# Four raw-weight buffers in place of two, in a one-core decoder trunk

## The chip, the core and the metric

The kernel runs on one core of a Trainium2 chip. The core has a matrix engine (TensorE, PE in the profile), a vector engine (VectorE, DVE), a scalar engine (ScalarE, ACT), a general engine (GpSimd, POOL) and a queue engine (SyncE, SP) that here only issues DMA transfers. Each runs its own list of instructions in order and waits on semaphores for the others. Sixteen DMA engines carry data between memory (HBM) and the on-chip buffer (SBUF, 128 partitions). Matrix products end in PSUM banks.

The metric is the device time of one execution in microseconds. Before the change the median of three runs is 2399.63 us (2398.58 to 2399.67).

## The reference

The input is one sequence of 512 vectors of 1024 float32 numbers, and a memory of 256 such vectors. Two layers follow each other. Each is: half a SwiGLU feed-forward step (FFN), a mixing step, half an FFN.

```python
def _swiglu(t, w_gate, w_up, w_down):
    return (jax.nn.silu(t @ w_gate) * (t @ w_up)) @ w_down
...
    for l in range(DEPTH):
        f = _swiglu(_rmsnorm(h, ffn1_pre_g[l]), ffn1_w_gate[l], ffn1_w_up[l], ffn1_w_down[l])
        h = h + 0.5 * _rmsnorm(f, ffn1_post_g[l])

        u = _rmsnorm(h, mix_pre_g[l])
        proj = u @ w_in[l]
...
        merged = (g_sb * (_merge_heads(o_sb) @ w_br_sb[l])
                  + g_fx * (_merge_heads(o_fx) @ w_br_fox[l])
                  + g_mem * (_merge_heads(o_mem) @ w_br_mem[l]))
        h = h + _rmsnorm(merged @ w_out[l], mix_post_g[l])

        f = _swiglu(_rmsnorm(h, ffn2_pre_g[l]), ffn2_w_gate[l], ffn2_w_up[l], ffn2_w_down[l])
        h = h + 0.5 * _rmsnorm(f, ffn2_post_g[l])
```

The FFN is 2816 wide (22 tiles of 128). The mixing step has eight heads of stick-breaking attention, eight of forgetting attention (a softmax with a decay) and four of attention to the memory, each gated by a sigmoid of a projection. All weights are float32 and are used once, so every weight comes from HBM in the course of the execution.

## The kernel before

**The arithmetic.** A float32 operand is split into a high part, rounded to the matrix engine's format, and the low part that remains. ScalarE makes the high part (line 188: `wh_...`, or 191 with a scale), VectorE subtracts it from the operand for the low part (line 189: `wl_...`, or 192). A product is then three matmuls of 128x128 by 128x512: high by high (line 214), low by high (215), high by low (216), added in PSUM. Activations are split in the same way.

**Units of weights.** Weights come in units of 512 KB: a `Unit` holds four row tiles by 256 columns, a `BlockUnit` two row tiles by 512 columns. `fetch` takes a tile with the tag "raw" and issues its DMA on SyncE's queue (line 262, and 313 for blocks); `load` makes the two halves and thereby frees the raw tile. A unit feeds 12 matmuls. The halves have four buffers each ("wh", "wl").

**Two by two blocks in seven products.** Most of the FFN's matrices are multiplied as two by two blocks by a scheme with seven block products in place of eight. Its operands are sums of blocks. Those of the weights are made on VectorE from a raw block and *kept* blocks (tiles kt for gate and up, bt for down), which are fetched on the same queue without the raw limit: product 2 subtracts a raw block from kept block 0 (line 337), product 3 takes the difference of the kept blocks (340), product 5 subtracts a raw block (345), product 6 as well (349); products 0 and 1 split a raw block as it is, and product 4 a kept block. In names, `wl_tc1_8_2_2` is the low part for FFN c1, group 8, product 2, second unit. The four FFNs are a0, c0, a1, c1 (layer 0 before and after mixing, layer 1 likewise), so the profile, which leaves numbers out, has ta, da, ga and tc, dc, gc.

**Stages of an FFN.** First two feature tiles, whose weights have buffers of their own, are multiplied plainly; then plain gate products of tiles 18 and 19 and the sums of the activations; then four groups of gate and up, of seven products each (the first in the order 0 to 6, the others 0, 2, 3, 4, 5, 1, 6), then two down products of seven each, with plain gate and up units of tiles 18 to 21 (named g..18, u..18, g..20, u..20) between, then the rest of down. In the first FFN the first group is followed by the statistics of the memory's norm (`mem_stats`, lines 1076 to 1084: squares and roots on ScalarE, which load activation tables). Between the FFNs the mixing stage multiplies plain units (w_in, gates wg and wb, w_out as wo, memory projections mk and mv) and runs the attention heads, whose exponentials and sums lie on ScalarE and VectorE.

**What sets the order.** A `Queue` holds jobs in program order. When a job starts, its units and those of the next jobs (up to four units ahead) are loaded. After each load, `fetch_ahead` goes through the jobs that follow and fetches raw units until as many are under way as the table `BUFS` has raw buffers (line 438); then it stops, and kept blocks of later units wait with it. So the count of raw buffers is used twice: in the tile pool, where a new raw tile waits for the tile that had its place, and here.

The lists that the engines run are not in the order of the program text: the build that allocates the tiles also places each engine's instructions by its own model of when each is ready. Only what `keep_in_program_order` or `in_order` (line 166) ties together keeps its order. On SyncE, each transfer that waits holds all that stand behind it.

**The scratch of dynamic transfers.** A part of SBUF is set aside for transfers that GpSimd issues. Its size is an argument of the program's constructor, left at its default here. The kernel has three such transfers, of small vectors, near the start: `bfor` (line 161) and two for `vecs` (lines 123 and 124), used in products at 62 us.

Of the kernel before, what the change touches and what calls it, by code (L numbers as in the profile page):

```python
# [22 lines left out]
def kernel(  # L23
# [38 lines left out]
    nc = tc.nc  # L62
# [37 lines left out]
    def tmp(name):  # L100
        return sb.tile([P, S], F32, tag="f32t", bufs=5, name=name)

    BUFS = {"u": 2, "v": 6, "q": 2, "k": 2, "o": 8, "tri": 2, "raw": 2, "rs": 1, "cs": 1, "wh": 4, "wl": 4, "f": 4}

    def stile(shape, tag, name, dt=F32R):
        return sb.tile(shape, dt, tag=tag, bufs=BUFS[tag], name=name)

# [264 lines left out]
    class Queue:  # L372
# [60 lines left out]
        def fetch_ahead(self):  # L433

            for units, _, _ in self.jobs[self.at:]:
                for un in units:
                    if un.waits():
                        if un.ring() and self.fetched == BUFS["raw"]:
                            return
# [1327 lines left out]
```

## Time and profile before

| | before |
|---|---|
| median of 3 runs | 2399.63 us |
| profiled execution, its own time | 2399.02 us |
| its span in the profile | 2397.3 us |
| TensorE busy | 2369.5 us, 99% |
| VectorE busy | 1870.9 us, 78% |
| ScalarE busy | 1399.4 us, 58% |
| GpSimd busy | 73.9 us, 3% |
| moved by DMA | 349.73 MB, 146 GB/s in the mean |
| share of the 16 DMA engines taken by SyncE's queue | 45.6% |
| granted TensorE clock | 0.999 |

The span runs from the first instruction to the last; the execution's own time has 1.7 us more, which lie outside it. The rows of a timeline have the start in us from the span's start, the duration in us, the engine, the line, the operation, output and inputs, and in brackets how long the engine had been idle before, and for what it waited. The rows of the waits have the engine, what waited, what ended the wait, and then the total in us, the number of times and the longest. "SPq" is SyncE's DMA queue.

### The profile page before, as it was taken

To read this page: it belongs to the slowest core of one execution; us is meant where nothing else is said; L and a number is where in the kernel's file an instruction comes from. 1 tells how busy PE (TensorE), PEld (TensorE's weight loads), DVE (VectorE), ACT (ScalarE), POOL (GpSimd) and SP (SyncE) were. 2 spreads that over 40 slices of the span, in tenths; PEclk is the share of its full clock that TensorE was granted. 3 is DMA by queue.
4 is the path that set the end of the run, shared out by engine and by line. 5 is a ranking of instruction groups with operands and counts; after the bars stand their busy time and mean duration, and the time that the engine had idled before them with its cause. 6 is when DMAs were issued, how large, how long until landed. Compare 5 with 4: busy or idle time off the path is not lost.

```text
span 2397.3 us, 31090 instructions
## 1 busy us (share of the span) xinstructions
PE 2369.5 (99%) x11688; PEld 1996.4 (83%) x11688; DVE 1870.9 (78%) x2532; ACT 1399.4 (58%) x2291; POOL 73.9 (3%) x130
## 2 busy tenths in 40 slices
PE   9999999999999999999999999999999999999998
PEld 8788788888888897888888887888888888888887
DVE  7778977678776687789787789776777766877895
ACT  5656555577665455565655565656675655555654
POOL 1000000001010000000000000000001100000000
PEclk9999999999999999999999999999999999999999
DMA  5464475222223445554645545642232244446454
GB/s 181 154 218 160 151 253 158 70 77 75 79 71 115 143 139 182 183 183 157 220 147 165 186 158 196 219 129 80 63 89 80 71 134 147 159 150 202 158 168 166
DMA packets 232603, 349.73 MB, mean 146 GB/s; under 512 B 10730, under 2 KB 117506, under 8 KB 231940
## 3 DMA queue, kind: packets, MB, share of 16 engines
q1 hardware_dynamic: 232352, 347.71, 45.6%
q8 instruction: 92, 1.51, 0.3%
q14 instruction: 59, 0.48, 0.1%
q0 software_dynamic: 96, 0.03, 0.0%
q10 hardware_dynamic: 4, 0.00, 0.0%
HBM read 333.02 MB, written 14.68 MB: 145 GB/s over the span
## 4 chain that ended last, share of the span: by engine, by line
PE 80%; DVE 8%; DMA 6%; ACT 3%; issue 2%; SPq 0%; DVEq 0%; ACTq 0%
PE pg L214 3%; PE pg L216 3%; PE pg L215 3%; PE ptc L215 3%; PE ptc L214 3%; PE ptc L216 3%; PE pta L214 3%; PE pta L215 3%; PE pta L216 3%; PE pdc L216 2%; PE pdc L215 2%; PE pdc L214 2%; PE pb L214 2%; PE pb L215 2%; PE pb L216 2%
## 5 line engine op out<-in xcount | busy, mean ns | idle before, releaser
L214 PE MATMUL pg<-us_a,wh_wg 128*128 128x512 f32 x384 | 151.0, 393 | 0.0
L216 PE MATMUL pg<-us_a,wl_wg 128*128 128x512 f32 x384 | 149.7, 390 | 0.0
L215 PE MATMUL pg<-us_a,wh_wg 128*128 128x512 f32 x384 | 149.6, 390 | 0.0
L188 ACT CAST wh_tc<-ktc 128x1024 fp32r<-128x1024 f32 x80 | 83.4, 1052 | 98.6 <-DVE ktc L349 34.1
L188 ACT CAST wh_ta<-kta 128x1024 fp32r<-128x1024 f32 x80 | 83.4, 1053 | 96.9 <-DVE kta L337 31.7
L189 DVE TENSOR_TENSOR wl_ta<-kta,wh_ta 128x1024 fp32r<-128x1024 f32 x80 | 97.1, 1222 | 29.8 <-ACT wh_ta L188 29.0
L189 DVE TENSOR_TENSOR wl_tc<-ktc,wh_tc 128x1024 fp32r<-128x1024 f32 x80 | 97.1, 1222 | 29.2 <-ACT wh_tc L188 28.4
L214 PE MATMUL pta<-wh_ta,aga 128*128 128x512 f32 x256 | 101.1, 397 | 4.5 <-ACT wh_ta L188 2.3
L214 PE MATMUL ptc<-wh_tc,agc 128*128 128x512 f32 x256 | 100.1, 393 | 3.1 <-ACT wh_tc L188 3.1
L215 PE MATMUL ptc<-wl_tc,agc 128*128 128x512 f32 x256 | 100.0, 391 | 1.5 <-DVE wl_tc L189 1.5
L215 PE MATMUL pta<-wl_ta,aga 128*128 128x512 f32 x256 | 100.2, 391 | 1.0 <-DVE wl_ta L189 1.0
L216 PE MATMUL pta<-wh_ta,aga 128*128 128x512 f32 x256 | 99.8, 391 | 0.0
L216 PE MATMUL ptc<-wh_tc,agc 128*128 128x512 f32 x256 | 99.4, 389 | 0.0
L215 PE MATMUL pda<-wl_da,aha 128*128 128x512 f32 x224 | 87.6, 391 | 0.8 <-DVE wl_da L189 0.8
L215 PE MATMUL pdc<-wl_dc,ahc 128*128 128x512 f32 x224 | 87.3, 390 | 0.5 <-DVE wl_dc L189 0.5
L214 PE MATMUL pda<-wh_da,aha 128*128 128x512 f32 x224 | 87.7, 391 | 0.1
L214 PE MATMUL pdc<-wh_dc,ahc 128*128 128x512 f32 x224 | 87.4, 390 | 0.0
L216 PE MATMUL pda<-wh_da,ala 128*128 128x512 f32 x224 | 86.9, 389 | 0.0
L216 PE MATMUL pdc<-wh_dc,alc 128*128 128x512 f32 x224 | 86.9, 389 | 0.0
L216 PEld LDWEIGHTS pg<-us_a,wl_wg 128*128 128x128 f32 x384 | 72.1, 188 | 15.3
L215 PEld LDWEIGHTS pg<-us_a,wh_wg 128*128 128x128 f32 x384 | 72.2, 188 | 14.1
L214 PEld LDWEIGHTS pg<-us_a,wh_wg 128*128 128x128 f32 x384 | 72.1, 188 | 14.1
(543 smaller groups left out, 7513.2 us busy)
## 6 DMA issues: line engine op xcount, KB each, us to landing
raw_ta<-in_ffn_w_gate_dram SPq DMA_DIRECT2D x64, 512.0 KB, 3.8
raw_tc<-in_ffn_w_gate_dram SPq DMA_DIRECT2D x64, 512.0 KB, 3.8
raw_da<-in_ffn_w_down_dram SPq DMA_DIRECT2D x58, 512.0 KB, 4.0
raw_dc<-in_ffn_w_down_dram SPq DMA_DIRECT2D x58, 512.0 KB, 3.5
raw_wg<-in_w_gate_dram SPq DMA_DIRECT2D x48, 512.0 KB, 3.6
kta<-in_ffn_w_up_dram SPq DMA_DIRECT2D x32, 512.0 KB, 5.4
ktc<-in_ffn_w_up_dram SPq DMA_DIRECT2D x32, 512.0 KB, 5.7
raw_wo<-in_w_out_dram SPq DMA_DIRECT2D x24, 512.0 KB, 3.4
```

What stands on the lines that cost most here:

```text
L188: both = [nc.scalar.copy(h_ap, src)]
L189: make = lambda: nc.vector.tensor_tensor(l_ap, src, h_ap.bitcast(F32), ALU.subtract)
L214: nc.tensor.matmul(pt, lh, rh, start=start, stop=False, skip_group_check=free)
L215: nc.tensor.matmul(pt, lh, rl, start=False, stop=False, skip_group_check=free)
L216: nc.tensor.matmul(pt, ll, rh, start=False, stop=stop, skip_group_check=free)
```

## The change

The raw tag has four buffers in place of two, so the pool holds four raw tiles of 4 KB per partition, and the limit on fetches under way (line 438) is four as well. The 8 KB per partition that this takes come from the scratch of dynamic transfers, which has 2 KB left. Nothing else in the text of the kernel differs; the order in which the build places the instructions of each engine is made anew.

```diff
-    BUFS = {"u": 2, "v": 6, "q": 2, "k": 2, "o": 8, "tri": 2, "raw": 2, "rs": 1, "cs": 1, "wh": 4, "wl": 4, "f": 4}
+    BUFS = {"u": 2, "v": 6, "q": 2, "k": 2, "o": 8, "tri": 2, "raw": 4, "rs": 1, "cs": 1, "wh": 4, "wl": 4, "f": 4}
...
-    nc = _bacc.Bacc("TRN2", target_bir_lowering=False, num_devices=1)
+    nc = _bacc.Bacc("TRN2", target_bir_lowering=False, num_devices=1, dynamic_dma_scratch_size=2048)
```

## The prediction

> **What bounds the kernel now.** I read the page's first two parts, then the chain that ended last:
>
> ```profile
> span 2397.3 us, 31090 instructions
> PE 2369.5 (99%) x11688; PEld 1996.4 (83%) x11688; DVE 1870.9 (78%) x2532; ACT 1399.4 (58%) x2291; POOL 73.9 (3%) x130
> ...
> PE 80%; DVE 8%; DMA 6%; ACT 3%; issue 2%; SPq 0%; DVEq 0%; ACTq 0%
> ```
>
> TensorE is busy in all but 2397.3 - 2369.5 = 27.8 us, and the change takes no matmul away. So 27.8 us, or a little more (below), is all that more buffers can win. The next view, the waits of TensorE alone, says what those microseconds waited for (columns: who, for whom; us in total, times, longest):
>
> ```profile
> PE ptc L214 <- ACT wh_tc L188: 3.1, 2, 2.2
> PE ptc L215 <- DVE wl_tc L189: 2.8, 3, 1.5
> PE pta L215 <- DVE wl_ta L189: 2.4, 3, 1.0
> PE pta L214 <- ACT wh_ta L188: 2.3, 2, 1.5
> PE pta L214 <- ACT ca L751: 2.2, 2, 1.2
> ...
> PE pga L216 <- DVE wl_ga L189: 1.4, 2, 0.7
> ...
> PE pgc L216 <- DVE wl_gc L189: 1.1, 2, 0.6
> PE pda L215 <- DVE wl_da L189: 0.8, 3, 0.3
> PE pqm L215 <- DVE us_a L192: 0.5, 1, 0.5
> PE pdc L215 <- DVE wl_dc L189: 0.5, 1, 0.5
> ```
>
> The eight rows with wh_ or wl_ are waits for a weight split in two (ACT makes the high part, DVE the low). They add to 3.1 + 2.8 + 2.4 + 2.3 + 1.4 + 1.1 + 0.8 + 0.5 = 14.4 us, in 18 places. The ca row is another thing (memory statistics on ACT), and pqm another (a norm).
>
> Are those splits late because of the raw buffers? The waits of SyncE's DMA queue:
>
> ```profile
> SPq L262 <- DVE wl_wg L192: 175.9, 34, 13.8
> ...
> SPq L313 <- DVE wl_tc L189: 99.6, 32, 10.9
> ```
>
> Every fetch of raw weights (L262, L313) waits for the DVE split that frees one of the two raw buffers, and whatever stands behind it in the queue, the kept blocks kta and ktc among it, waits too. The largest place, in the first group of the second FFN (c0):
>
> ```profile
> 903.91 1.23 DVE L337 TENSOR_TENSOR ktc<-ktc,raw_tc 128x1024 f32<-128x1024 f32 x1 [2.72 <-DMA raw_tc<-in_ffn_w_gate_dram]
> ...
> 908.53 1.22 DVE L340 TENSOR_TENSOR ktc<-ktc,ktc 128x1024 f32<-128x1024 f32 x1
> ```
>
> ```profile
> 909.86 1.04 ACT L188 CAST wh_tc<-ktc 128x1024 fp32r<-128x1024 f32 x1 [0.17 <-DVE ktc L340]
> ```
>
> ```profile
> 908.35 0.39 PE L216 MATMUL ptc<-wh_tc,us_b 128*128 128x512 f32 x1
> 910.96 1.15 PE L214 MATMUL ptc<-wh_tc,agc 128*128 128x512 f32 x3 [2.23 <-ACT wh_tc L188]
> ```
>
> Read upwards: TensorE waits 2.23 us for the cast, that for the DVE sum, and DVE had lost 2.72 us waiting for a raw block to land. Another place of the kind, in the last FFN:
>
> ```profile
> 2160.39 0.37 SPq L313 DMA_DIRECT2D raw_tc<-in_ffn_w_gate_dram  x1
> 2162.75 0.37 SPq L313 DMA_DIRECT2D raw_tc<-in_ffn_w_gate_dram  x1
> ```
>
> ```profile
> 2161.50 1.23 DVE L189 TENSOR_TENSOR wl_tc<-raw_tc,wh_tc 128x1024 fp32r<-128x1024 f32 x1
> 2166.63 1.23 DVE L337 TENSOR_TENSOR ktc<-ktc,raw_tc 128x1024 f32<-128x1024 f32 x1 [3.91 <-DMA raw_tc<-in_ffn_w_gate_dram]
> ...
> 2171.31 1.22 DVE L760 TENSOR_TENSOR cc<-cc,cc 128x1024 f32<-128x1024 f32 x1
> 2172.44 1.22 DVE L340 TENSOR_TENSOR ktc<-ktc,ktc 128x1024 f32<-128x1024 f32 x1
> 2173.58 1.22 DVE L189 TENSOR_TENSOR wl_tc<-ktc,wh_tc 128x1024 fp32r<-128x1024 f32 x1
> ```
>
> ```profile
> 2172.71 0.39 PE L216 MATMUL ptc<-wh_tc,agc 128*128 128x512 f32 x1
> 2172.94 0.39 PE L214 MATMUL ptc<-wh_tc,agc 128*128 128x512 f32 x1
> 2174.85 0.50 PE L215 MATMUL ptc<-wl_tc,agc 128*128 128x512 f32 x1 [1.53 <-DVE wl_tc L189]
> 2175.19 0.39 PE L216 MATMUL ptc<-wh_tc,agc 128*128 128x512 f32 x1
> ```
>
> The raw block left only at 2160.39, when a split freed a buffer; DVE then idled 3.91 us for it, and TensorE paid 1.53 us at 2174.85. These rows also price a wait in full: from 2172.94 to 2175.19 two steps took 2.25 us, where the step before took 0.23, so the loss is 2.25 - 0.46 = 1.79: the wait, and 0.26 us more in the restart.
>
> **The change, part by part.** (1) *Two more raw buffers.* The planner's limit (L438) reads the same table, so four units of 512 KB may be under way. A fetch now waits for a split two units older. One unit feeds 4 x 3 matmuls at the step of 0.23 us above, 2.8 us, so fetches may leave up to 5.5 us earlier. In both places shown that exceeds DVE's idle time for the DMA (2.72 and 3.91), and the kept blocks behind them move forward too. Expected to go are all 18 waits, less a part of one: in the first FFN's first group DVE is short of time, not of data:
>
> ```profile
> 53.99 1.23 DVE L337 TENSOR_TENSOR kta<-kta,raw_ta 128x1024 f32<-128x1024 f32 x1 [0.44 <-DMA raw_ta<-in_ffn_w_gate_dram]
> ...
> 60.11 1.22 DVE L189 TENSOR_TENSOR wl_ta<-kta,wh_ta 128x1024 fp32r<-128x1024 f32 x1
> ```
>
> There DVE waited 0.44 us for DMA, and TensorE 1.5 (the longest of the pta L214 row), so about 0.5 goes and 1.0 stays. Gain: 14.4 - 1.0 = 13.4 us of waits, and 17 restarts x 0.26 = 4.4: **17.8 us**. Its lower bound is what DVE's own idle time explains alone (the first rival, 6 us); the upper end is 14.4 + 18 x 0.26 = 19.1.
>
> (2) *The order changes with it.* The build arranges each engine's instructions by its own modelled times. Numbers of instructions and transfers stay; some 390 of DVE's rows and 245 of ACT's stand elsewhere, about 100 of TensorE's, 66 of SyncE's and none of POOL's. What moves:
>
> (2a) *DVE: the L337 of the next group goes ahead of the low split of product 6 of the current one.* There are 16 places (three group changes in each of four FFNs, and one in each down product). Before, in the down product of the first FFN:
>
> ```profile
> 252.79 1.23 DVE L349 TENSOR_TENSOR bta<-bta,raw_da 128x1024 f32<-128x1024 f32 x1 [0.73 <-DMA raw_da<-in_ffn_w_down_dram]
> ...
> 255.21 1.23 DVE L189 TENSOR_TENSOR wl_da<-bta,wh_da 128x1024 fp32r<-128x1024 f32 x1
> ```
>
> ```profile
> 260.30 0.39 PE L215 MATMUL pda<-wl_da,aha 128*128 128x512 f32 x1
> ```
>
> The split starts at 255.21 and its first matmul at 260.30: 5.1 - 1.2 = 3.9 us to spare. An L337 that is ready costs 1.2 of it: nothing. One that waits for its block as long as the worst row (3.91 us) costs 3.91 + 1.23 - 3.9 = 1.2 us on TensorE; where the second L337 waits too, its own 1.2 and a restart of 0.26 come on top, 2.7 us. Per place 0 to 2.7, in all 0 to 43 (a gain is excluded: this wait is new). The raw block of such an L337 now leaves about 5.5 us earlier, which is more than 3.91, so the nearest value is 0; I take 2 us for a few misses.
>
> (2b) *ACT: the memory statistics of the first FFN go some 16 us earlier.* They cause the ca row:
>
> ```profile
> 109.19 0.57 ACT L751 COPY ca<-pta 128x512 f32<-128x512 f32 x1
> 109.78 1.28 ACT L1084 ACT_TABLE_LOAD   x1
> ```
>
> The same table loads of 1.28 us now stand before casts of product 2 instead of before the copies that free ca. Bounds: both waits go (-2.2 - 0.5 for restarts), or the casts behind a statistics tile that has not landed lose as much again (+2.7). Nothing tells which; I take 0.
>
> (2c) *Borders between stages.* Splits of the next stage's first weights (the gate projections, the w_out and memory projections, the plain FFN units) stand before norms and transposes that a chain of dependent work needs, at about twelve borders. The nearest row is pqm, 0.5 us in one place, and no other border has such a wait. A split on DVE ahead of a chain costs 1.2 us where nothing covers it, so 0 to 14 (12 x 1.2); cover is the earlier stage's matmuls. I take 12 x 0.25 = 3 us.
>
> (2d) *SyncE.* Gains, reloads and stores go behind raw fetches in its one queue; the issues are under half a microsecond each (0.37 above) and are used many units later. TensorE starts product 3 of a first group before product 2 and takes product 0 of a later group 24 matmuls later, which is cover for the splits. First FFNs do two raw splits (2.4 us) ahead of the sums on the activations; cover is the 12 matmuls of each unit. I take 1 us, bounds 0 and 4 x 2.4 = 10.
>
> (3) *The scratch shrinks to 2 KB.* Only POOL's transfers use it:
>
> ```profile
> q0 software_dynamic: 96, 0.03, 0.0%
> ```
>
> 96 packets, three transfers near the start, none of them in a wait of TensorE above. Nothing; if a ring too short made one of them two landings long, cover is the first FFN.
>
> Sum: -17.8 + 2 + 0 + 3 + 1 = -11.8 us on the profiled execution. That one took 2399.02, 1.7 us more than its span and 0.6 less than the median of the three runs; 2399.0 - 11.8 = **2387 us**.
>
> **The rivals.** *Covered: DVE is the limit, not the data.* In front of several of the waits DVE does not idle: from 2171.31 to the end of the split of 2173.58 it works without a gap. If only waits with DVE idle for a DMA close before them go, those are the two shown and two or three like them: 2.2 + 1.5 + about 1 and 5 restarts = 6 us, and (2) takes its 6. Then 2399, within 0.2%, say 2395 to 2404. For it: DVE is 78% busy. Against it: the gaps of 2.72 and 3.91 us are lost DVE time that the queued work behind inherits.
>
> *Slower: the early L337 holds DVE.* At each of the 16 places of (2a) the subtraction waits in order for its block, and the split behind it comes late. At the upper price of (2a), 2.7 us a place, it decides from (17.8 - 4 + 4.8) / 2.7 = 7 places on, where the time passes 2404. With eight, 2399.0 - 17.8 + 4 + 21.6 = 2407 us. For it: transfers slow each other, and the one issued at 2160.39 was used only at 2166.63 (6.2 us), and with two more units under way more traffic stands ahead of each. Against it: its slot comes free 5.5 us earlier. The Trainium skill, "Perfetto Trace Analysis", section "Tensor Engine Instruction (MATMUL, LD_WEIGHTS)", calls ACT and DVE strict FIFO; by that rule nothing overtakes the waiting subtraction and this rival is possible, and the trace agrees: no DVE row stands in the 3.91 us before 2166.63.
>
> *It does nothing:* the limit on fetches does not bind. The rows of SyncE's waits (175.9 us in 34 times) speak against that; 2399 us.
>
> **How the numbers follow.** About 0.2%, 4.8 us, is what a measurement of this kernel can tell from no change. Forecast 2387 (2381 to 2394 with its own bounds: all of the gain and the ca row, 2399 - 19.1 - 2.7 + 4, to half of the gain lost to (2)): chance 0.64. Covered: 0.18, 2399. Slower by the early L337: 0.16, 2407. Nothing: 0.02, 2399. So faster 0.64, same 0.20, slower 0.16. The range leaves out about one in ten above and less below: 2381 to 2405.
>
> **What would show it.** TensorE's waits: the eight rows fall from 14.4 to under 4 us, ptc L214 first of all. SyncE's raw fetches wait for splits two units older, and DVE's waits for raw blocks at L337 fall. Wrong (2a): a DVE row of L337 with a DMA wait, and behind it a TensorE wait for wl of product 6. Wrong (2b): TensorE waiting for wh near 95 to 100 us. Wrong (2c): new rows of us_, fb or ts among TensorE's waits. The prediction is wrong at its root if TensorE's waits fall and its steps grow longer instead, or if most of the waits stay with DVE busy before them.

## The result and the profile after

The changed kernel takes 2375.52 us (median of four runs, 2374.8 to 2376.61) against 2399.65 for the kernel before (four runs): ratio 0.99, 95% interval 0.9883 to 0.9917. Timed again later beside two other kernels it took 2375.88, ratio 0.9904 (0.9889 to 0.9919). It is faster by 24 us, twice the forecast of 12, and below the range of 2381 to 2405.

The page of the changed kernel, its span, its engines and its chain:

```profile
span 2373.9 us, 31089 instructions
PE 2362.5 (100%) x11688; PEld 1997.1 (84%) x11688; DVE 1868.3 (79%) x2532; ACT 1412.3 (59%) x2292; POOL 73.9 (3%) x130
...
PE 97%; DVE 2%; ACT 1%; DMA 0%; issue 0%; DVEq 0%; SPq 0%; ACTq 0%
```

DMA had 6% of the chain and has none; TensorE had 80% and has 97%. All that TensorE still waits for:

```profile
PE pts L1204 <- ACT ts L1235: 1.5, 2, 0.7
PE warm L1637 <- DVE warm L1721: 1.3, 1, 1.3
PE ptc L215 <- DVE wl_tc L189: 0.5, 1, 0.5
PE pga L818 <- ACT us_x L191: 0.4, 1, 0.4
PE pta L215 <- DVE wl_ta L189: 0.4, 1, 0.4
PE pga L818 <- ACT w_ga L188: 0.2, 1, 0.2
PE pda L216 <- DVE ala L189: 0.2, 1, 0.2
```

The eight rows of waits for split weights, 14.4 us before, have shrunk to 0.5 + 0.4 = 0.9. A ninth row of the kind before, `PE pga L214 <- ACT wh_ga L188: 0.4, 2, 0.2`, which the prediction's sum leaves out, is gone too. So are the ca row and the pqm row. The rows that stay are the program's start (warm, pga) and the attention (pts), which have nothing to do with raw weights. The first group of c0, where TensorE waited 2.23 us before product 3, now runs like this (VectorE's timeline, then TensorE's):

```profile
890.86 1.22 DVE L189 TENSOR_TENSOR wl_tc<-raw_tc,wh_tc 128x1024 fp32r<-128x1024 f32 x1
892.00 1.22 DVE L337 TENSOR_TENSOR ktc<-ktc,raw_tc 128x1024 f32<-128x1024 f32 x1
893.13 1.22 DVE L189 TENSOR_TENSOR wl_tc<-ktc,wh_tc 128x1024 fp32r<-128x1024 f32 x1
894.38 1.22 DVE L340 TENSOR_TENSOR ktc<-ktc,ktc 128x1024 f32<-128x1024 f32 x1
```

```profile
899.72 0.39 PE L216 MATMUL ptc<-wh_tc,us_b 128*128 128x512 f32 x1
899.94 0.39 PE L214 MATMUL ptc<-wh_tc,agc 128*128 128x512 f32 x1
900.17 0.39 PE L215 MATMUL ptc<-wl_tc,agc 128*128 128x512 f32 x1
```

No bracket stands at L337, so the raw block was there, and the products on the sums (agc) begin one step of 0.22 us after the last plain one.

One trace is not the whole story. The later timing left a second trace of the same kernel, with a span of 2375.6 us, and in it one wait for a low half is longer:

```profile
PE pta L215 <- DVE wl_ta L189: 2.1, 2, 1.7
```

So two traces of one kernel differ by 1.7 us of span; the place of that wait is shown further down, at (2a).

**Where the 23.4 us of span went.** The waits listed for TensorE fell from 20.9 us in 28 places to 4.5 in 8, that is 16.4. TensorE's busy time fell from 2369.5 to 2362.5, 7.0 us, with the same 11688 matmuls: the first matmul after a stall is longer and the next one follows later (at 2174.85 in the prediction's rows 0.50 and 0.34 us, in place of 0.39 and 0.23), and the profile counts that as work. 16.4 + 7.0 = 23.4, the whole difference of the spans (2397.3 - 2373.9). In the second trace it is 15.2 + 6.5 = 21.7.

### The profile page after: what moved, and what is told of

It reads as the page before. It is cut to its first block, busy times and chain, and to the rows that moved or that the text cites. A ratio compares the mean times of both kernels' runs of the same rounds, so it can differ in the third digit from the quotient of the medians.

```text
span 2373.9 us, 31089 instructions
## 1 busy us (share of the span) xinstructions
PE 2362.5 (100%) x11688; PEld 1997.1 (84%) x11688; DVE 1868.3 (79%) x2532; ACT 1412.3 (59%) x2292; POOL 73.9 (3%) x130
## 4 chain that ended last, share of the span: by engine, by line
PE 97%; DVE 2%; ACT 1%; DMA 0%; issue 0%; DVEq 0%; SPq 0%; ACTq 0%
PE pta L215 4%; PE pta L214 4%; PE pta L216 4%; PE ptc L214 4%; PE ptc L215 4%; PE ptc L216 4%; PE pg L214 4%; PE pg L216 4%; PE pg L215 4%; PE pdc L216 3%; PE pdc L214 3%; PE pdc L215 3%; PE pda L216 3%; PE pda L215 3%; PE pda L214 3%; PE pb L214 2%
## 5 line engine op out<-in xcount | busy, mean ns | idle before, releaser
L214 PE MATMUL pg<-us_a,wh_wg 128*128 128x512 f32 x384 | 151.0, 393 | 0.0
L215 PE MATMUL pg<-us_a,wh_wg 128*128 128x512 f32 x384 | 149.6, 390 | 0.0
L188 ACT CAST wh_tc<-ktc 128x1024 fp32r<-128x1024 f32 x80 | 84.3, 1054 | 64.3 <-PE ptc L216 34.5
L188 ACT CAST wh_ta<-kta 128x1024 fp32r<-128x1024 f32 x80 | 84.2, 1053 | 55.6 <-PE pta L216 30.4
L189 DVE TENSOR_TENSOR wl_tc<-ktc,wh_tc 128x1024 fp32r<-128x1024 f32 x80 | 97.7, 1222 | 23.4 <-ACT wh_tc L188 23.2
L189 DVE TENSOR_TENSOR wl_ta<-kta,wh_ta 128x1024 fp32r<-128x1024 f32 x80 | 97.6, 1221 | 21.7 <-ACT wh_ta L188 21.5
L214 PE MATMUL pta<-wh_ta,aga 128*128 128x512 f32 x256 | 100.3, 392 | 0.1
L214 PE MATMUL ptc<-wh_tc,agc 128*128 128x512 f32 x256 | 100.3, 392 | 0.0
L215 PE MATMUL pta<-wl_ta,aga 128*128 128x512 f32 x256 | 99.7, 390 | 0.4 <-DVE wl_ta L189 0.4
L215 PE MATMUL ptc<-wl_tc,agc 128*128 128x512 f32 x256 | 99.7, 389 | 0.0
L214 PE MATMUL pdc<-wh_dc,ahc 128*128 128x512 f32 x224 | 87.4, 390 | 0.0
L214 PE MATMUL pda<-wh_da,aha 128*128 128x512 f32 x224 | 87.3, 390 | 0.0
L215 PE MATMUL pda<-wl_da,aha 128*128 128x512 f32 x224 | 87.2, 389 | 0.0
L215 PE MATMUL pdc<-wl_dc,ahc 128*128 128x512 f32 x224 | 87.2, 389 | 0.0
L215 PEld LDWEIGHTS pg<-us_a,wh_wg 128*128 128x128 f32 x384 | 72.2, 188 | 14.1
L214 PEld LDWEIGHTS pg<-us_a,wh_wg 128*128 128x128 f32 x384 | 72.1, 188 | 14.1
```

Source lines behind the costliest of these rows:

```text
L188: both = [nc.scalar.copy(h_ap, src)]
L189: make = lambda: nc.vector.tensor_tensor(l_ap, src, h_ap.bitcast(F32), ALU.subtract)
L214: nc.tensor.matmul(pt, lh, rh, start=start, stop=False, skip_group_check=free)
L215: nc.tensor.matmul(pt, lh, rl, start=False, stop=False, skip_group_check=free)
```

## The experiments

The theory was that a raw block's place in the pool comes free too late, so its transfer leaves too late, and TensorE waits for the split. The rivals were the planner's limit, the order of instructions that the build makes anew, the memory that moves, and any deeper buffer on the way. Each run was timed beside the kernel before on one chip; there single executions of the kernel before took 2393.4 to 2404.6 us, and their medians lay between 2396.9 and 2399.4, so the ratios are what to read. In all runs but two (the scratch alone, and the order of before) the build makes the order of instructions anew.

**The scratch alone.**

```diff
-    nc = _bacc.Bacc("TRN2", target_bir_lowering=False, num_devices=1)
+    nc = _bacc.Bacc("TRN2", target_bir_lowering=False, num_devices=1, dynamic_dma_scratch_size=2048)
```

> Two raw buffers as before, and only the scratch of dynamic transfers cut to 2 KB; the order on every engine is that of before. If the gain comes from the raw buffers: 2399 to 2400 us, the time of before. If the smaller scratch or the addresses that move with it have a part in it: below 2396.

Measured 2399.2 us, ratio to before 1.0005 (0.9993 to 1.0018). No effect of the smaller scratch shows.

**The pool without the limit.** The changed kernel, and at line 438:

```diff
-                        if un.ring() and self.fetched == BUFS["raw"]:
+                        if un.ring() and self.fetched == 2:
```

> Four raw tiles in the pool, but the planner's limit on fetches under way stays at two. If the pool's places do the work (a fetch waits for the split that frees its place, wherever the program text puts it): 2375 to 2378 us, and the order is nearly that of the changed kernel. If the planner's limit does it: about 2399, or in between if both count.

Measured 2376.77 us, ratio 0.9904 (0.9884 to 0.9924), the time of the changed kernel. The program text is that of before, apart from the size of the pool and of the scratch. So the planner's limit is not what binds: the place in the pool is. The build itself moves fetches ahead of their position in the text: SyncE's order in this trace differs from that of the changed kernel in 8 of 666 transfers, from that of before in 53.

**Three buffers.**

```diff
-"raw": 4,
+"raw": 3,
```

> Three raw buffers, pool and limit. The head start of a fetch is one unit (2.8 us) in place of two. Theory of the head start: TensorE's waits for splits fall from 14.4 us to about half (places with a DMA gap under 2.8 us close, the largest ones stay in part), 2383 to 2390 us. If any third buffer lifts the limit whole: 2375 to 2378. If only the fourth does it: over 2395.

Measured 2384.0 us, ratio 0.9939 (0.9921 to 0.9957), about 15 us of the 24. TensorE's waits for splits in it:

```profile
PE pta L215 <- DVE wl_ta L189: 4.4, 4, 2.1
...
PE pta L214 <- ACT wh_ta L188: 1.2, 1, 1.2
```

5.6 us are left of 14.4, in five places of the first FFN; one more buffer closes the rest. The forecast of this run, 2383 to 2390 us, holds.

**The order of before with four buffers.** The kernel of the second experiment, in which each engine's instructions (all but POOL's, whose order did not change) are tied one behind the other in the order that the build gave them in the kernel before; `_ORDER` holds that order, packed:

```diff
+def _old_order(nc, tc):
+    traced = {i.name: i for i in nc.cur_bb.bb.instructions}
...
+            if prev is not None:
+                tc.add_manual_dep(i, prev.name, nosync, reason="in_order")
+            prev = i
...
         tile_macaron_trunk_kernel(tc, *args)
+        _old_order(nc, tc)
```

> Four raw buffers, but every engine's instructions tied to the order of the kernel before, line for line. It tells the buffers from the order that the build makes with them. If the earlier transfers are the cause: TensorE's waits for splits mostly go, 2376 to 2384 us; the waits for ca (memory statistics, 2.2 us) stay. If the new order (subtractions earlier, TensorE's products in first groups exchanged) is the cause: over 2392 us.

Measured 2377.39 us, ratio 0.9906 (0.9887 to 0.9926). TensorE's waits:

```profile
PE pts L1204 <- ACT ts L1235: 1.5, 2, 0.7
PE warm L1637 <- DVE warm L1721: 1.3, 1, 1.3
PE pta L214 <- ACT ca L751: 0.7, 1, 0.7
PE pta L214 <- ACT wh_ta L188: 0.7, 2, 0.4
PE ptc L214 <- ACT wh_tc L188: 0.5, 2, 0.2
PE pga L818 <- ACT us_x L191: 0.4, 1, 0.4
```

VectorE's waits for raw blocks at the sums were 61.4 us in 53 places before. All that is left of them here:

```profile
DVE btc L349 <- DMA raw_dc<-in_ffn_w_down_dram: 1.5, 2, 0.9
DVE bta L349 <- DMA raw_da<-in_ffn_w_down_dram: 1.0, 2, 0.5
```

This is the run that decides. With the old order on every engine, line for line, 21.6 of the 23.4 us of span are gained (2397.3 - 2375.7). So nine tenths of the gain or more is transfers, of raw and of kept blocks, that leave and land earlier. The last 1.8 us can't be put down to the new order, since the two traces of the changed kernel differ by as much. One part of the expectation failed: the ca waits were to stay, and fell from 2.2 to 0.7 us.

**Kept blocks early, raw blocks as before.** Two raw buffers and the small scratch; the fetch of a unit is cut in two, one for the kept blocks and one for the raw block, each with a limit of its own. By these rules two and two with two buffers would be the kernel before, four and four with four buffers the changed one; neither was run in this form.

```diff
+                    if keep and not un.kept and un.h is None:
+                        if un.ring() and self.kept == 4:
+                            keep = False
+                        else:
+                            un.fetch_keep()
+                    if raw and un.waits():
+                        if un.ring() and self.fetched == 2:
+                            raw = False
+                        else:
+                            un.fetch_raw()
```

> Two raw buffers as before, but the kept blocks (kt, bt) are requested as early in the program as in the changed kernel, ahead of the raw fetches that wait. It tells whether the loss came from kept blocks stuck behind waiting raw fetches or from the raw blocks themselves. If the raw blocks are the cause (DVE's gaps end on raw blocks in the rows): 2392 to 2400 us, with the waits at products 2 left and those at product 3 smaller. If the kept blocks are: under 2384.

Measured 2407.65 us, ratio 1.0041 (1.0029 to 1.0053): slower by 10 us, which neither theory had expected. VectorE in the first group of the first FFN (L355 is L337 there), and TensorE's longest waits:

```profile
54.74 1.22 DVE L355 TENSOR_TENSOR kta<-kta,raw_ta 128x1024 f32<-128x1024 f32 x1 [1.19 <-DMA raw_ta<-in_ffn_w_gate_dram]
57.31 1.23 DVE L355 TENSOR_TENSOR kta<-kta,raw_ta 128x1024 f32<-128x1024 f32 x1 [1.34 <-DMA raw_ta<-in_ffn_w_gate_dram]
```

```profile
PE pta L214 <- ACT wh_ta L188: 5.7, 3, 3.4
PE ptc L214 <- ACT wh_tc L188: 3.8, 2, 2.0
PE pda L215 <- DVE wl_da L189: 3.7, 5, 0.8
```

The kept blocks are there; the raw ones are what VectorE waits for. Blocks that could have waited now travel ahead of raw blocks that can't. The worst place of each FFN is the first subtraction of its second group. In the third FFN (a1) it was so before (SyncE's issue, then VectorE; the matching rows):

```profile
1276.58 0.37 SPq L313 DMA_DIRECT2D raw_ta<-in_ffn_w_gate_dram  x1
```

```profile
1280.35 1.23 DVE L337 TENSOR_TENSOR kta<-kta,raw_ta 128x1024 f32<-128x1024 f32 x1 [1.47 <-DMA raw_ta<-in_ffn_w_gate_dram]
```

and is so in this run (L329 is L313):

```profile
1276.86 1.49 SPq L329 DMA_DIRECT2D kta<-in_ffn_w_up_dram  x3
1281.13 2.70 SPq L329 DMA_DIRECT2D raw_ta<-in_ffn_w_gate_dram  x2
```

```profile
1288.09 1.23 DVE L355 TENSOR_TENSOR kta<-kta,raw_ta 128x1024 f32<-128x1024 f32 x1 [4.64 <-DMA raw_ta<-in_ffn_w_gate_dram]
```

Three kept blocks are issued just ahead of the raw one, which is used 7.0 us after its issue in place of 3.8. In the other three FFNs the raw block of this place takes 5.4 to 6.2 us in place of 3.7 to 4.0, and VectorE waits 3.0 to 4.0 us in place of 1.5 to 1.8. So the transfers do slow each other here; how much of the 10 us that makes was not traced.

**Raw blocks early, kept blocks as before.** Four raw buffers, and the limits of the run above exchanged (`self.kept == 2`, `self.fetched == 4`).

> The other half: four raw buffers, but kept blocks are requested only when the two-unit limit of before would have let them. If the raw blocks are the cause: 2376 to 2382 us. If the kept blocks have to come early too: over 2388. With the run before it, this splits the 23 us: the two gains add up if the causes are separate, and each alone gives less than its share if both have to be there.

Measured 2380.21 us, ratio 0.9933 (0.9918 to 0.9948), about 16 us of the 24. VectorE now waits for the other operand:

```profile
DVE kta L355 <- DMA kta<-in_ffn_w_up_dram: 11.5, 7, 3.3
...
DVE bta L355 <- DMA bta<-in_ffn_w_down_dram: 8.7, 7, 2.7
```

Raw early alone gives 16, kept early alone costs 10, both together give 24. The two don't add up: kept blocks early pay only when raw blocks are early too.

**The statistics elsewhere.** The kernel before, with the statistics of the memory's norm behind the last group in place of the first:

```diff
             Q.add([], vectors)
-            Q.add([], lambda: iter(mem_stats() or ()))
...
             later[:] = over
+        if name == "a0":
+            Q.add([], lambda: iter(mem_stats() or ()))
         todo = downs(0)
```

> The kernel before, with the statistics of the memory's norm moved in the program from behind the first group to behind the last. It isolates the two ca waits (2.2 us). If those waits are caused by the table loads on ACT: they go, and with 0.3 to 0.5 us for each restart the time falls by 2.5 to 4 us, to about 2395 to 2396. If they are a consequence of late weights around them: under 1 us.

Measured 2396.71 us, ratio 1.0 (0.9991 to 1.0009). The row of ca waits is gone, and yet the time is not shorter, since other waits have grown: in this profile `pta L214 <- ACT wh_ta` 4.2 us (2.3 before) and `pda L215 <- DVE wl_da` 2.2 (0.8 before) are among them. The run does not price the ca waits. Its order was made anew as well (616 of VectorE's 2532 instructions stand elsewhere), so it does not show whether a wait that is removed at one place comes back at others while weights are short, or whether the new order brought these.

**A price for a wait.** The changed kernel, with the low half of product 4's first unit made five times over in each gate-and-up group, the same values each time, 16 places:

```diff
         both.append(make())
+        for _ in range(again):
+            both.append(make())
...
-            self.split_from(src)
+            self.split_from(src, again=4 * (self.n == 4 and self.k0 == 0 and self.pair is not None))
```

> The changed kernel, with the low split of product 4's first unit in every gate-and-up group made five times over (the same values), 16 places, each 4 x 1.14 = 4.6 us later. It prices a wait of TensorE by itself: by the difference of the two profiles, each wait should cost its listed idle time and 0.3 to 0.4 us for the restart. If the listed idle time were the whole price, time over waits would be 1.0; with restarts of 0.3 to 0.4 and waits of 1 to 2 us, 1.2 to 1.4. If the slack at these places is over 4.6 us, nothing changes, and the price stays open.

Measured 2390.32 us, ratio 0.9966 (0.9953 to 0.9979). The waits for splits and one of the places (L217 is L215 here):

```profile
PE pta L217 <- DVE wl_ta L189: 7.2, 4, 3.6
PE ptc L217 <- DVE wl_tc L189: 2.7, 2, 1.4
```

```profile
921.07 0.50 PE L217 MATMUL ptc<-wl_tc,agc 128*128 128x512 f32 x1 [1.35 <-DVE wl_tc L189]
921.40 0.40 PE L218 MATMUL ptc<-wh_tc,agc 128*128 128x512 f32 x1
921.64 0.39 PE L217 MATMUL ptc<-wl_tc,agc 128*128 128x512 f32 x1
```

Two things follow. TensorE was stopped in at most six of the 16 places, so in ten or more a split that is 4.6 us later still is in time. How much of this reserve two buffers had was not measured. And the span grew by 2388.8 - 2373.9 = 14.9 us where the listed waits of TensorE grew by 10.7 (4.5 to 15.2), 1.4 times the waits, as in the comparison of before and after (23.4 / 16.4 = 1.4). At the place shown, the next step is 0.33 us in place of 0.23, and the wait is counted only from the modelled end of the matmul before (0.39 us after its start, where the step is 0.23): 0.16 and 0.10, the 0.26 us of the forecast. So 0.26 is right for one plain wait; the rest of the 4.2 us was not traced to its places.

**A fifth raw buffer.** The changed kernel with `"raw": 5`; the memory just holds it.

> Five raw buffers; the memory just holds them beside 2 KB of scratch. With four, TensorE waits only 0.9 us in two places for splits, and its other waits have nothing to do with weights. So if head start is the cause, the fifth adds at most 1 to 1.5 us: within 0.1% of the changed kernel. If the gain still grows with every buffer (7 us from the third to the fourth): 2370 or less.

Measured 2375.08 us, ratio to before 0.9901 (0.9884 to 0.9917), beside 0.9904 for four. No more is gained, as the 0.9 us of waits that were left say; the two can't be told apart.

**Halves in place of raw buffers.** The kernel before with the small scratch, five high and five low tiles, and five units of look-ahead:

```diff
-"wh": 4, "wl": 4,
+"wh": 5, "wl": 5,
...
-        AHEAD = 4
+        AHEAD = 5
```

> Two raw buffers as before, and the 8 KB given to the halves instead: five high and five low tiles, and the planner loads five units ahead. If any deeper buffer on the way of the weights would do: 2375 to 2385 us. If the transfers must leave earlier (theory): a split can only be early if its raw block is there, so 2390 to 2400 us.

Measured 2383.72 us, ratio 0.9937 (0.9922 to 0.9952): 15 us faster, where 2390 to 2400 had been expected. This is a miss of the theory in its narrow form. TensorE's largest waits there:

```profile
PE pta L214 <- ACT ca L751: 1.8, 1, 1.8
PE pts L1204 <- ACT ts L1235: 1.5, 2, 0.7
PE pta L214 <- DVE ca L753: 1.5, 2, 1.2
...
PE pta L215 <- DVE wl_ta L189: 0.8, 1, 0.8
```

The waits for splits are almost gone here too. The same with the look-ahead left at four (the second line of the diff undone):

> As the run with five halves, but the planner still loads four units ahead, so the program text is that of before and only the tile pool differs. If the pool's places do the work there too (a split that finds a free half runs earlier, frees its raw tile earlier, and the next transfer leaves earlier): 2383 to 2386 us. If the fifth unit of look-ahead did it: 2394 to 2400.

Measured 2386.78 us, ratio 0.9946 (0.9929 to 0.9962). So most of it needs no change of the planner either. A likely reason is that a split that finds a free half can run earlier, and so frees its raw place earlier. The traces agree in size. Count for each fetch and each split of the tiles ta, tc, da and dc how many matmuls TensorE had begun by then, at 0.23 us each, and compare the first with the first, the second with the second: against before, raw fetches leave 2.9 us earlier in the median (2.4 with the look-ahead left at four), and low halves are ready 2.7 us earlier (2.5), about one unit of 2.8. VectorE still waits 48 us for raw blocks (46), against 61 before; it does so further ahead of TensorE. So the raw buffers are one of two places where the loop from fetch to split can be made deeper, and the better one here.

## Why the prediction was wrong

**The mechanism was right.** *Part (1)*, the eight rows of waits for splits: forecast 14.4 to 1.0, measured 14.4 to 0.9. The slots in the pool bring it (the pool with the old limit, 0.9904), the transfers and not the order carry it (old order, 0.9906), and no cost of the scratch shows, as *part (3)* said. They are not the only thing that would: five halves with two raw buffers left 1.0 us of these rows. And the head start was sized too low. Counted in matmuls begun, as for the halves, raw fetches leave 8.2 us earlier in the median with the old order, and 12.5 in the changed kernel, in place of up to 5.5. Two of the seven products take no raw block, so two raw blocks stand for 2 x 7/5 = 2.8 units, an estimate of 7.8 us.

**The step that failed is the allowance of (2), (2c) and (2d) above all, and with it the bound of the range.** The sum gave back 2 + 3 + 1 = 6 us to waits that the new order would bring. The first trace has 0.7 us of them, 0.5 in the way of (2a) and 0.2 in the only new row, `pda <- ala`; the second has 1.7 and 0.4. And ca and pqm, for which the sum took nothing, went.

- *(2a), the L337 ahead of product 6's split, 2 us.* The early subtractions do wait for their blocks in the changed kernel:

```profile
DVE ktc L337 <- DMA raw_tc<-in_ffn_w_gate_dram: 8.7, 8, 2.1
...
DVE kta L337 <- DMA raw_ta<-in_ffn_w_gate_dram: 8.0, 6, 2.8
...
DVE bta L337 <- DMA raw_da<-in_ffn_w_down_dram: 5.1, 4, 1.5
...
DVE btc L337 <- DMA raw_dc<-in_ffn_w_down_dram: 4.7, 4, 1.4
```

  The longest is 2.8 us in this trace and 3.2 in the second, under the 3.9 to spare that had been worked out from 255.21 and 260.30, and no wl of product 6 is among TensorE's waits. But the work behind inherits the loss, and in one place of each trace it reached TensorE one product later, at the first unit of the next group. In the first trace:

```profile
2088.55 1.23 DVE L337 TENSOR_TENSOR ktc<-ktc,raw_tc 128x1024 f32<-128x1024 f32 x1 [2.08 <-DMA raw_tc<-in_ffn_w_gate_dram]
```

```profile
2098.24 0.50 PE L215 MATMUL ptc<-wl_tc,us_b 128*128 128x512 f32 x1 [0.46 <-DVE wl_tc L189]
```

  and in the second:

```profile
1252.88 1.22 DVE L337 TENSOR_TENSOR kta<-kta,raw_ta 128x1024 f32<-128x1024 f32 x1 [3.25 <-DMA raw_ta<-in_ffn_w_gate_dram]
```

```profile
1262.64 0.49 PE L215 MATMUL pta<-wl_ta,us_c 128*128 128x512 f32 x1 [1.71 <-DVE wl_ta L189]
```

  Between the two rows of each pair VectorE has one more gap, at the second L337 (0.31 and 0.39 us), and then none up to the split that TensorE waits for. Each place is without a wait in the other trace, where its two L337 waited 0.7 and 0.6, and 1.0 and 0.5 us. (Before, every FFN waited 0.6 to 0.7 us at this unit, with no L337 ahead of its split.) The Trainium skill, "Perfetto Trace Analysis", section "Tensor Engine Instruction (MATMUL, LD_WEIGHTS)", calls VectorE strict FIFO; by that rule an L337 that waits holds all that stands behind it, and the trace agrees: no row of VectorE stands in the 2.08 us before 2088.55. At 1.4 us of time for each listed one (the run with late low halves) the price is an estimate of 0.6 and 2.4 us, so the 2 us of (2a) were not far off. The slower rival needed at least seven places and had one in each trace. Its argument that transfers slow each other is borne out: with the old order raw blocks of the FFNs' gates and downs land in 4.3 to 4.6 us in the median, against 3.5 to 4.0 before; but that is much less than they leave earlier.
- *(2b), the statistics, 0 us of -2.7 to +2.7.* Both ca waits went, 2.2 us and their restarts. Most of that needs no moving of the statistics: with the old order they fell to 0.7.
- *(2c), the borders, 3 us, and (2d), 1 us.* In the first trace `pda <- ala` came with 0.2 us, in the second also `pwo <- wl_wo` with 0.2; the one that was there, pqm with 0.5 us, went. Such rows come and go without a new order: the run with the scratch alone, in the order of before, has 2.0 us of them at the norms (utx, utc).

**The other part is the price of restarts.** 17 times 0.26 made 4.4 us; TensorE's busy time fell by 7.0 over 20 places, 0.35 each. The plain wait costs what the row said (0.26, seen again in the run with late low halves), but other places lose more; in the first group of c0 before, this row of TensorE's timeline stands behind the ones shown in the prediction:

```profile
911.94 0.39 PE L215 MATMUL ptc<-wl_tc,agc 128*128 128x512 f32 x1
```

The four steps from 908.35 to 911.94 took 3.59 us where four of 0.23 take 0.92, so 2.67 were lost, 0.44 more than the wait of 2.23.

Together, for the first trace: forecast -11.8, and then -1.5 for (2a), -3.8 for (2c) and (2d), -2.2 for ca, -0.5 for pqm, -0.4 for the ninth row, -0.6 because the first FFN's first group kept 0.4 us in place of 1.0, and -2.6 for restarts. That is -23.4, as measured.

**The range** missed for the same reason. Its lower end took the whole gain, 19.1, and the ca row, 2.7, and then added 4 us of new waits even to the best case. The rows allowed zero for each of these, so the best case of its own bounds was 2399 - 21.8 = 2377, and with the pqm row and the measured restarts 2375.

**The rival that VectorE is the limit** falls. Its argument was that VectorE works without a gap just before several of the waits. That is so, but at 2171.31 the work was late because it stood behind the gap of 3.91 us for DMA that ended at 2166.63; where the blocks land earlier and the order stays (the old order), TensorE has no wait for a low half left, and 1.2 us of waits for high ones. VectorE is 79% busy after, 78% before.

## What to carry to other kernels

When the bound engine waits a little in many places, go back from each wait past the engine that is busy just before it, to the last gap: the busy stretch is often only late, and the gap says by what. Two buffers hide a transfer only if the one who frees them is on time; here a third gave 15 of 24 us, a fourth the rest and a fifth nothing that could be told, a fifth pair of halves in their place gave 15 as well, and memory for it lay in a scratch that the kernel hardly used. An allowance for waits that no row shows should widen the range upward, not shift the sum and both ends.

## What was not expected of the hardware

- More transfers early is not better by itself: kept blocks requested earlier, with raw blocks as before on the same queue, made the kernel 10 us slower (1.0041, 1.0029 to 1.0053). A raw block with three kept blocks just ahead of it was used 7.0 us after its issue, in place of 3.8.
- A wait of TensorE costs more than its listed idle time: 1.4 times as much over all, in two comparisons (23.4 for 16.4 us, 14.9 for 10.7), and 0.26 us of the difference is seen at each plain wait: the idle time is counted from a modelled end of the matmul before (0.39 us after its start, with starts 0.23 us apart), and the step behind the first matmul after it is 0.1 us longer. That makes 5.2 of the 7.0 us over 20 places; the rest was not traced. The Trainium skill, "Perfetto Trace Analysis", section "Tensor Engine Instruction (MATMUL, LD_WEIGHTS)", says that TensorE's end times are estimated and not observed; the trace agrees, in that busy time fell by 7.0 us for the same 11688 matmuls.
